# Last round of an MLP: a plain chunk ahead of the pair of a seven-product and a plain chunk, and final norm's row loaded in the last chunk

## The chip, the cores and the metric

The kernel runs on one core of one Trainium2 chip. The metric is the device time of one execution in microseconds; times of a kernel are given as the median of three runs. The engines are TensorE (PE, matrix products; PEld are its weight loads), VectorE (DVE), ScalarE (ACT), GpSimd (POOL) and SyncE (SP), whose queue issues the transfers from and to HBM.

## The reference, cut to what matters

One decoder layer on 256 tokens of 2048 features in float32: two groups of attention heads, an output projection, and then an MLP of four times the width, with norms and residual adds. The change lies in the MLP and in the last norm:

```python
h = rms_norm(x, norm2_g[l])
x = x + jnp.square(jax.nn.relu(h @ w_mlp_in[l])) @ w_mlp_out[l]
...
return rms_norm(x, final_norm_g)
```

## The kernel before

All products are made with operands that are split into a high and a low part (float32r): hi x hi, lo x hi and hi x lo, three matrix instructions for one product. A weight block is loaded from HBM by SP into a buffer raw (1 MB, 512 rows of 512 columns; four buffers), and split in two *steps* of 256 rows each: ACT writes the high part whi (L252), DVE subtracts and writes the low part wlo (L253). The tiles for these parts come from a ring of five (wsplit has four, late5 the fifth), so that a split of a step can begin when PE has done the step five before it.

The weights are cut into *chunks* of 512 output columns. The MLP has four rounds (r = 0 to 3). In each, four chunks "u" (up projection, features on the partitions, L414) make 2048 hidden features, and four chunks "d" (down projection, d(r,0) to d(r,3)) multiply them by 2048 rows of w_mlp_out and add to the residual xs. A d chunk of eight steps is done in one of two ways:

- *plain*: product(), L397 to L399, into two accumulators "acc", one per token tile (128 tokens). There are four acc banks, so a chunk works in two while the two before are drained. drain_d adds them to xs on DVE (L808).
- as a *seven-product* (seven_products(), L457): a Strassen-like form of the 2 x 2 block product with seven products in place of eight. It needs sums and differences of the weights (L207, L222, L223 on DVE) and of the hidden activations (mix_activations and split_mixed, L743 to L746 and mix_hi, mix_lo), and all four banks called sc and tr. drain_seven takes it to xs in four parts, on slots 1, 3, 5 and 7 behind its end (L784 to L792 and L777); its copies tile, its both, fhi and flo and the mix_hi and mix_lo tiles lie in a pool "late".

One seven-product chunk, d(r-1,0), is woven into the four u chunks of the next round, a quarter (a *unit* of four steps near, first, odd, even) to each. d(r,1) is woven with the plain d(r,2) in the same way, four units of six steps: this is the *pair*. d(r,3) is plain. In the last round d(3,0) is plain too, since no u chunks follow.

The order of the steps is written out in the list steps (L147 to L158). A *slot* is half a step, 128 rows of the weights; side work is hung on slots with at(slot, function). e is the slot of a chunk's last step. When a slot's products are issued, run_side issues its side work, so on each engine the drains stand in the queue between the splits of the steps ahead. How far ahead the splits go is set by free_tiles and, near the end, by upto (L946); load_more keeps up to four raw buffers in use.

The last chunk, d(3,3), is written by last_chunk (L846): first all of token tile 0, then tile 1 in two halves of 256 columns. The high and low parts of its first three steps go to the tiles aT_hi and aT_lo, which the u chunks have done with. For the final norm each piece of xs is squared and summed on ACT when its last add is done (square_and_gain, L802), and multiplied by the gain row gf on DVE (put_gain, L820). load_gf (L757) closes the pool "late", takes gf (8 KB on each partition, the same 2048 values on all) in its place, and loads it on SP's queue; so it has to wait until the last readers of that pool are done. finish computes the norm's factor for a token tile from the sums (POOL for the power, L833), scales the tile on DVE and ACT (L841, L843), and sends it out on SP (L844).

In the last round before the change the order is: four u chunks with d(2,0); the pair d(3,1) and d(3,2); plain d(3,0); plain d(3,3). The drains of the pair, load_gf and put_gain for columns 512 to 1535 are hung on slots of d(3,0).

Of the kernel before, what the change touches and what calls it, by code (L numbers as in the profile page):

```python
# [28 lines left out]
CW = 512  # L29
# [45 lines left out]
def kernel(  # L75
# [51 lines left out]
    ROUNDS = D_FF // D_MODEL  # L127
# [8 lines left out]
    steps = [(ci, s, "") for ci in range(mlp0) for s in range(chunks[ci][6] // 2)]  # L136
# [4 lines left out]
    def plain(ci):  # L141
        return [(ci, s, "") for s in range(KT // 2)]

    def mixed(ci, unit, behind):
        b, a, t13, t24 = ((ci, 2 * unit, sub) for sub in ("near", "first", "odd", "even"))
        return [b, a, t13, behind[0], t24] + behind[1:]

    for r in range(ROUNDS):
        for c in range(4):
            mine = plain(index["u", (r, c)])  # L150
            steps += mine[:4] + (mixed(index["d", (r - 1, 0)], c, mine[4:]) if r else mine[4:])
        late = [index["d", (r, c)] for c in range(4)]
        if r < ROUNDS - 1:
            steps += plain(late[3])
        for unit in range(4):
            steps += mixed(late[1], unit, plain(late[2])[2 * unit:2 * unit + 2])
        if r == ROUNDS - 1:
            steps += plain(late[0]) + plain(late[3])  # L158

    last_slot = {chunks[ci][:2]: 2 * i + 1 for i, (ci, _, _) in enumerate(steps)}  # L160
    units = list(dict.fromkeys((ci, s // 2) for ci, s, _ in steps))
# [311 lines left out]
    def at(i, f, *a):  # L473
        side.setdefault(i, []).append((f, a))
# [293 lines left out]
    def drain_seven(r, c, ci, part):  # L768
# [28 lines left out]
        if r == ROUNDS - 1 and part % 2:  # L797
            square_and_gain(part // 2, cs, c)

    def square_and_gain(t, cs, n):  # L800
        unused = two.tile([P, CW], F32, name="nat")
        nc.scalar.activation(unused[:, :cs.stop - cs.start], xs[:, t, cs], AF.Square, accum_out=ssq3[:, t, n:n + 1])  # L802
        if n not in (1, 2):
            put_gain(t, cs)

    def add_down(acc, t, cs, n):

        nc.vector.scalar_tensor_tensor(  # L808
            xs[:, t, cs], acc[:, :cs.stop - cs.start], rstd2sq[:, t:t + 1], xs[:, t, cs], op0=ALU.mult, op1=ALU.add
        )  # L810
        if n is not None:
            if cs.stop < D_MODEL:
                square_and_gain(t, cs, n)
            else:
                unused = two.tile([P, CW], F32, name="nat")
                unused, xc, total = unused[:, :cs.stop - cs.start], xs[:, t, cs], ssq3[:, t, n:n + 1]
                nc.vector.tensor_tensor_reduce(unused, xc, xc, 1.0, 0.0, ALU.mult, ALU.add, total)

    def put_gain(t, cs):
        nc.vector.tensor_tensor(xs[:, t, cs], xs[:, t, cs], late_tiles["gf"][:, cs], op=ALU.mult)  # L820
# [51 lines left out]
    for ci, (what, key, *_rest) in enumerate(chunks[:-1]):  # L872
        e = last_slot[what, key]
        if what == "v":
            at(e, drain_v, key, ci)
            if key == 0:
                at(e + 2, forget_gates)
                at(e + 6, gate_sums)
                at(e + 4, rel_row)
                at(e + 5, rel_back)  # L880
                at(e + 55, rel_turn)
        elif what in "qk":
            for half in range(2):
                late = half if what == "k" else (2 if key else 8) + 5 * half
                at(e + late, drain_qk, key, what, ci, half)
            if what == "k":
                kind = groups[key][4]
                for h in range(4):
                    n = e + 6 + 7 * (h // 2)
                    if kind == 0:  # L890
                        at(n - 3, decay_of, groups[key][3] * 4 + h)
                    at(n, scores, key, h)
                for h in range(4):
                    at(e + 20 + 7 * (h // 2), values, key, h)
                for h in range(4):
                    at(e + 13 + 7 * (h // 2), turn_probs, key, h)
                if key % 2:
                    at(e + 33, group_norm, kind)
        elif what == "o":
            at(e, drain_o, *key, ci)  # L900
            if key[0] == 1:
                for n in range(2):
                    at(e + 2, to_features, 4 * key[1] + 2 * n, 16)
                if key[1] == 3:
                    at(e + 4, second_norm)
        elif what == "u":
            at(e, drain_u, key[1], ci)
            at(e + 2, mix_activations, key[1])
            at(e + 4, split_mixed, key[1])
        elif ci in seven:  # L910
            for part in range(4):
                at(e + 1 + 2 * part, drain_seven, *key, ci, part)
            if key[0] == ROUNDS - 1:
                at(e + 7, load_gf)
                for c in (1, 2):
                    for t in range(TB):
                        at(e + 11 + 2 * c + t, put_gain, t, slice(c * CW, (c + 1) * CW))
        else:
            at(e, drain_d, *key, ci)

# [31 lines left out]
    for i in range(final):  # L952
        if i == mlp_start:
# [3 lines left out]
            late = late_forms.enter_context(tc.tile_pool(name="late", bufs=1))  # L957
# [58 lines left out]
```

## Time and profile before

| | us |
|---|---|
| median of three runs | 1099.67 |
| the three runs | 1099.06, 1099.67, 1099.78 |
| profiled execution, its own time | 1097.77 |
| its span, first to last instruction | 1096.0 |
| PE busy in the span | 1080.1 |
| DVE busy | 800.7 |
| ACT busy | 604.1 |
| last round: last u product (995.42) to last chunk (1064.47) | 69.05 |
| last chunk: token tile 0 | 10.88 |
| last chunk: tile 1, two halves | 5.75 and 5.96 |
| from the last product to the end of the span | 8.94 |

Rows of a timeline have the start and the length of an instruction in us, the engine, the line, the operation, the tile written and the tiles read, the sizes, and in square brackets how long the engine was idle before it and who ended that. Rows of who waited for whom have the sum, the number and the longest of the waits. A row of "windows" has a stretch, its length and the busy time and instruction count of each engine in it, then the TensorE clock granted (1.00 is full) and the share and rate of the DMA engines.

### The profile page before, as it was taken

What the parts mean: (1) busy time and instruction counts of PE and PEld (TensorE: products, weight loads), DVE (VectorE), ACT (ScalarE), POOL (GpSimd) and SP (SyncE); (2) the same over time, 40 slices, a digit from 0 to 9 for tenths busy, and PEclk for the clock granted to TensorE, in tenths of its full rate; (3) what the DMA queues carried; (4) which work ended last, traced back from release to release, by engine and by line L of the source; (5) the groups of instructions that cost most, each with busy time, mean ns of one, the idle gap of its engine ahead of it and who ended that gap; (6) DMA issues with size and microseconds to landing.
All of it is one profiled execution on the core that took longest, in us unless ns stands there. A gap on an engine that the chain in (4) does not pass through costs nothing.

```text
span 1096.0 us, 19064 instructions
## 1 busy us (share of the span) xinstructions
PE 1080.1 (99%) x7877; PEld 1014.8 (93%) x7877; DVE 800.7 (73%) x1076; ACT 604.1 (55%) x821; POOL 27.9 (3%) x42
## 2 busy tenths in 40 slices
PE   9999999999999999999999999999999999998996
PEld 7999899998988899998999998999998899998886
DVE  6666756667576666578777789787778887779774
ACT  6455545546455565655546665546666556666541
POOL 0010200000001000000000000000000000000000
PEclk9999999999999999999999999999999999999999
DMA  8665464655545567646766554675665666655642
GB/s 319 235 217 169 155 200 146 193 177 170 193 154 192 165 188 224 193 158 207 216 196 199 205 203 158 206 218 187 197 212 173 194 197 186 193 196 180 215 178 77
DMA packets 105395, 209.27 MB, mean 191 GB/s; under 512 B 3971, under 2 KB 5084, under 8 KB 105180
## 3 DMA queue, kind: packets, MB, share of 16 engines
q1 hardware_dynamic: 104412, 206.59, 57.7%
q8 instruction: 61, 1.00, 0.4%
q0 software_dynamic: 304, 1.06, 0.3%
q10 hardware_dynamic: 592, 0.40, 0.1%
q14 instruction: 26, 0.21, 0.1%
HBM read 205.93 MB, written 2.11 MB: 190 GB/s over the span
## 4 chain that ended last, share of the span: by engine, by line
PE 98%; ACT 0%; DVE 0%; DMA 0%; issue 0%; POOL 0%; ACTq 0%; DVEq 0%
PE acc L414 48%; PE acc L397 11%; PE acc L398 11%; PE acc L399 11%; PE sc L457 7%; PE tr L457 5%; PE tr L349 1%; PE sc L676 1%; PE sc L632 1%; PE tr L660 0%; DMA xs<-in_x_dram 0%; PE sc L628 0%; ACT whi L252 0%; PE sc L678 0%; PE sc L398 0%
## 5 line engine op out<-in xcount | busy, mean ns | idle before, releaser
L253 DVE TENSOR_TENSOR wlo<-raw,whi 128x1024 fp32r<-128x1024 f32 (+2 forms) x327 | 394.5, 1221 | 162.0 <-ACT whi L252 161.1
L252 ACT ACTIVATE whi<-raw 128x1024 fp32r<-128x1024 f32 (+2 forms) x328 | 339.2, 1050 | 228.3 <-PE acc L414 129.9
L414 PE MATMUL acc<-aT_hi,whi 128*128 128x256 f32 x1536 | 425.6, 277 | 0.0
L414 PE MATMUL acc<-aT_hi,wlo 128*128 128x256 f32 x1536 | 424.1, 276 | 0.0
L414 PE MATMUL acc<-aT_lo,whi 128*128 128x256 f32 x1536 | 423.9, 276 | 0.0
L414 PEld LDWEIGHTS acc<-aT_hi,whi 128*128 128x128 f32 x1536 | 288.1, 188 | 1.2 <-issue 0.9
L414 PEld LDWEIGHTS acc<-aT_lo,whi 128*128 128x128 f32 x1536 | 288.2, 188 | 0.3
L414 PEld LDWEIGHTS acc<-aT_hi,wlo 128*128 128x128 f32 x1536 | 288.1, 188 | 0.1
L397 PE MATMUL acc<-whi,big_hi 128*128 128x512 f32 (+1 forms) x414 | 160.2, 387 | 0.0
L398 PE MATMUL acc<-whi,big_lo 128*128 128x512 f32 (+1 forms) x414 | 159.9, 386 | 0.0
L399 PE MATMUL acc<-wlo,big_hi 128*128 128x512 f32 (+1 forms) x414 | 159.8, 386 | 0.0
L399 PEld LDWEIGHTS acc<-wlo,big_hi 128*128 128x128 f32 x414 | 78.1, 189 | 15.8
L398 PEld LDWEIGHTS acc<-whi,big_lo 128*128 128x128 f32 x414 | 78.1, 189 | 14.4
L397 PEld LDWEIGHTS acc<-whi,big_hi 128*128 128x128 f32 x414 | 78.1, 189 | 14.2
L218 ACT ACTIVATE whi<-both 128x1024 fp32r<-128x1024 f32 x56 | 59.7, 1066 | 49.0 <-DVE both L223 17.1
L219 DVE TENSOR_TENSOR wlo<-both,whi 128x1024 fp32r<-128x1024 f32 x56 | 68.3, 1220 | 4.7 <-ACT whi L218 3.8
L336 DVE TENSOR_TENSOR big_lo<-nat,big_hi 128x512 fp32r<-128x512 f32 x32 | 22.1, 692 | 42.3 <-ACT big_hi L335 42.3
L397 PE MATMUL acc<-whi,aT_hi 128*128 128x512 f32 (+1 forms) x144 | 51.7, 359 | 0.0
L398 PE MATMUL acc<-whi,aT_lo 128*128 128x512 f32 (+1 forms) x144 | 51.0, 354 | 0.0
L399 PE MATMUL acc<-wlo,aT_hi 128*128 128x512 f32 (+1 forms) x144 | 51.0, 354 | 0.0
L218 ACT ACTIVATE whi<-raw 128x1024 fp32r<-128x1024 f32 x28 | 29.6, 1056 | 11.6 <-PE sc L457 5.0
L335 ACT ACTIVATE mix_hi<-nat 128x512 fp32r<-128x512 f32 x32 | 18.5, 625 | 29.9 <-DVE nat L745 29.9
(212 smaller groups left out, 1359.5 us busy)
## 6 DMA issues: line engine op xcount, KB each, us to landing
raw<-in_w_mlp_in_dram SPq DMA_DIRECT2D x64, 1024.0 KB, 5.6
raw<-in_w_mlp_out_dram SPq DMA_DIRECT2D x64, 1024.0 KB, 5.1
raw<-in_w_in_dram SPq DMA_DIRECT2D x42, 1024.0 KB, 5.2
raw<-in_w_out_dram SPq DMA_DIRECT2D x16, 1024.0 KB, 5.1
raw<-in_w_in_dram SPq DMA_DIRECT2D x4, 1040.0 KB, 9.5
xs<-in_x_dram SPq DMA_DIRECT2D x3, 512.0 KB, 9.5
raw<-in_w_in_dram SPq DMA_DIRECT2D x2, 512.0 KB, 5.3
big_lo<-rel_d POOLq DMA_DIRECT2D x1, 1024.0 KB, 7.1
```

Source lines behind the costliest of these rows:

```text
L218: nc.scalar.activation(hi, src, AF.Copy)
L219: nc.vector.tensor_tensor(lo, src, hi.bitcast(F32), op=ALU.subtract)
L252: nc.scalar.activation(hi[:, :, c:c + step], t[:, :, c:c + step], AF.Copy)
L253: nc.vector.tensor_tensor(lo, t, hi.bitcast(F32), op=ALU.subtract)
L335: nc.scalar.activation(hi, src, AF.Copy)
L336: nc.vector.tensor_tensor(lo, src, hi.bitcast(F32), op=ALU.subtract)
L349: nc.tensor.transpose(p[:, j * SEQ + t * P:j * SEQ + (t + 1) * P], xs[:, t, c:c + P], ident)
L397: nc.tensor.matmul(acc, xh, hi[:, j, cols], start=go, stop=False, skip_group_check=True)
L398: nc.tensor.matmul(acc, xl, hi[:, j, cols], start=False, stop=False, skip_group_check=True)
L399: nc.tensor.matmul(acc, xh, lo[:, j, cols], start=False, stop=end, skip_group_check=True)
L414: nc.tensor.matmul(acc, w[:, j, b * P:(b + 1) * P], a[:, kt, :], start=kt == 0 and b % 2 == 0 and n == 0, stop=kt == kts - 1 and n == 2, s ...
L457: nc.tensor.matmul(acc, a[:, k, tokens], w[:, j, n * half:(n + 1) * half], start=fresh and x == 0, stop=s == KT // 2 - 2 and j == 1 and x ...
```

## The change

In the last round the plain chunk d(3,0) comes ahead of the pair, as d(r,3) does in the other rounds; the pair is followed by the last chunk at once. The pair's drains, which hang on slots behind its end, fall into the last chunk, and with them load_gf (slot e + 7, which is the fifth of the last chunk's sixteen slots for token tile 0). put_gain for columns 0 to 1535 of both token tiles, six calls, hangs on slots e + 13 to e + 18, the last six of those sixteen; d(3,0) is no longer multiplied by gf at its drain, since gf is not there yet. Nothing else is changed: the products, the transfers and their sizes are the same.

```diff
@@ the order of the steps
         late = [index["d", (r, c)] for c in range(4)]
-        if r < ROUNDS - 1:
-            steps += plain(late[3])
+        steps += plain(late[3 if r < ROUNDS - 1 else 0])
         for unit in range(4):
             steps += mixed(late[1], unit, plain(late[2])[2 * unit:2 * unit + 2])
         if r == ROUNDS - 1:
-            steps += plain(late[0]) + plain(late[3])
+            steps += plain(late[3])
@@ square_and_gain
-        if n not in (1, 2):
+        if n > 2:
             put_gain(t, cs)
@@ side work of a seven-product chunk
             if key[0] == ROUNDS - 1:
                 at(e + 7, load_gf)
-                for c in (1, 2):
+                for c in range(3):
                     for t in range(TB):
-                        at(e + 11 + 2 * c + t, put_gain, t, slice(c * CW, (c + 1) * CW))
+                        at(e + 13 + 2 * c + t if t == 0 or c < 2 else e + 18, put_gain, t, slice(c * CW, (c + 1) * CW))
```

The changed file is one line shorter, so its line numbers behind the list of steps are one lower than those of before.

On PE, where the last product of the last u chunk (L414; L413 after the change) is followed by the first d products of the last round. Before:

```order
L414 MATMUL acc<-aT_lo,whi 128x256
L414 MATMUL acc<-aT_hi,wlo 128x256
L457 MATMUL sc<-whi,big_hi 128x256
L457 MATMUL sc<-whi,big_lo 128x256
L457 MATMUL sc<-wlo,big_hi 128x256
```

After:

```order
L413 MATMUL acc<-aT_lo,whi 128x256
L413 MATMUL acc<-aT_hi,wlo 128x256
L396 MATMUL acc<-whi,big_hi 128x512
L397 MATMUL acc<-whi,big_lo 128x512
L398 MATMUL acc<-wlo,big_hi 128x512
```

The seven-product's first step, into an sc bank, stood there; now the plain chunk's first step, into acc banks.

On SP's queue, the end of the program (raw are weight blocks, gf is final norm's row, out the output). Before:

```order
L177 DMA raw_11181<-in_w_mlp_out_dram 128x4x512
L177 DMA raw_11232<-in_w_mlp_out_dram 128x4x512
L760 DMA gf_11265<-in_final_norm_g_dram 128x2048
L177 DMA raw_11277<-in_w_mlp_out_dram 128x4x512
L844 DMA out_0_dram<-xs_87 128x384
```

After:

```order
L176 DMA raw_11153<-in_w_mlp_out_dram 128x4x512
L176 DMA raw_11201<-in_w_mlp_out_dram 128x4x512
L176 DMA raw_11251<-in_w_mlp_out_dram 128x4x512
L759 DMA gf_11385<-in_final_norm_g_dram 128x2048
L843 DMA out_0_dram<-xs_87 128x384
```

The load of gf stood ahead of the last weight block; now it stands behind all of them, and only outputs follow.

On DVE, from the last drains of the pair to the add of the last chunk's token tile 0 (L808 with acc; L807 after). Before, where the rows begin in d(3,0):

```order
L792 TENSOR_TENSOR tr<-tr,copies 128x256
L777 SCALAR_TENSOR_TENSOR xs<-sc,rstd2sq,xs 128x512
L253 TENSOR_TENSOR wlo_11249<-raw,whi_11248 128x1024
L777 SCALAR_TENSOR_TENSOR xs<-tr,rstd2sq,xs 128x512
L253 TENSOR_TENSOR wlo<-raw,whi 128x1024
L253 TENSOR_TENSOR aT_lo<-raw,aT_hi 128x1024 x3
L253 TENSOR_TENSOR wlo<-raw,whi 128x1024
L820 TENSOR_TENSOR xs<-xs,gf 128x512 x4
L253 TENSOR_TENSOR wlo<-raw,whi 128x1024 x2
L808 SCALAR_TENSOR_TENSOR xs<-acc,rstd2sq,xs 128x512
```

After, where all of them but the splits of the first six steps (the first two rows) stand behind the pair's end:

```order
L252 TENSOR_TENSOR aT_lo<-raw,aT_hi 128x1024 x3
L252 TENSOR_TENSOR wlo<-raw,whi 128x1024 x3
L785 TENSOR_TENSOR tr<-tr,copies 128x256
L776 SCALAR_TENSOR_TENSOR xs<-sc,rstd2sq,xs 128x512
L807 SCALAR_TENSOR_TENSOR xs<-acc,rstd2sq,xs 128x512 x2
L252 TENSOR_TENSOR wlo_11350<-raw,whi_11349 128x1024
L776 SCALAR_TENSOR_TENSOR xs<-tr,rstd2sq,xs 128x512
L776 SCALAR_TENSOR_TENSOR xs<-sc,rstd2sq,xs 128x256
L252 TENSOR_TENSOR wlo<-raw,whi 128x1024
L791 TENSOR_TENSOR tr<-tr,copies 128x256
L776 SCALAR_TENSOR_TENSOR xs<-sc,rstd2sq,xs 128x512
L776 SCALAR_TENSOR_TENSOR xs<-tr,rstd2sq,xs 128x512
```

The next row there is put_gain, L819, six in a row, then the two sums and the add of tile 0. The first put_gain waits for gf; before, the four at that place came between splits, half a chunk behind the load.

## The prediction

> **What bounds the kernel now.** I read the page first: the span, the busy shares and the chain that ended last.
>
> ```profile
> span 1096.0 us, 19064 instructions
> PE 1080.1 (99%) x7877; PEld 1014.8 (93%) x7877; DVE 800.7 (73%) x1076; ACT 604.1 (55%) x821; POOL 27.9 (3%) x42
> PE 98%; ACT 0%; DVE 0%; DMA 0%; issue 0%; POOL 0%; ACTq 0%; DVEq 0%
> ```
>
> TensorE (PE) works nearly all the time and 98% of the last chain is PE. The change leaves the matrix products as they are, so it can only move two things: places where PE waits, and the stretch after the last product. The list of who waited for whom, for PE from 400 us to the end, has one row:
>
> ```profile
> PE tr L457 <- DVE xs L777: 3.3, 1, 3.3
> ```
>
> The timelines of PE and of DVE show where it is: in the last round, in the first unit of the pair.
>
> ```profile
> 998.04 0.28 PE L457 MATMUL sc<-wlo,mix_hi 128*128 128x256 f32 x1
> 1001.61 0.38 PE L457 MATMUL tr<-whi,mix_hi 128*128 128x256 f32 x1 [3.29 <-DVE xs L777]
> 1000.81 0.74 DVE L777 SCALAR_TENSOR_TENSOR xs<-tr,rstd2sq,xs 128x512 f32<-128x512 f32 x1
> ```
>
> The pair's seven-product takes over all four sc and tr banks from the seven-product that ran beside the last u chunks. Its last drain (L777) stands on DVE behind the drains and splits of that u chunk and ends at 1001.55; PE, wanting the last tr bank, sits for 3.29 us. Windows then price this and the end: stretch, length, PE busy (instructions), the same for PEld, DVE, ACT and POOL, the granted clock, DMA share, GB/s.
>
> ```profile
> 998.04:1001.61 3.57, 0.28 (x4) 0.08 (x2) 2.78 (x5) 2.52 (x3) 0.00 (x0) 1.00 0.00 0
> 1001.61:1005.48 3.87, 3.87 (x15) 3.43 (x15) 3.77 (x7) 2.64 (x4) 0.00 (x0) 0.56 0.78 269
> 824.55:888.28 63.73, 63.73 (x362) 55.94 (x361) 52.66 (x59) 36.25 (x43) 0.00 (x0) 1.00 0.61 197
> 995.42:1064.47 69.05, 65.75 (x362) 57.38 (x361) 56.73 (x66) 39.73 (x51) 0.00 (x0) 0.98 0.55 190
> 1064.47:1075.35 10.88, 10.88 (x49) 9.01 (x48) 7.70 (x11) 3.35 (x6) 0.00 (x0) 1.00 0.01 2
> 1075.35:1081.10 5.75, 5.75 (x49) 5.75 (x48) 4.10 (x10) 0.72 (x1) 1.34 (x2) 1.00 0.12 44
> 1081.10:1087.06 5.96, 5.92 (x50) 5.72 (x48) 1.13 (x4) 0.51 (x2) 0.00 (x0) 1.00 0.35 133
> 1087.06:1096.00 8.94, 0.00 (x0) 0.00 (x0) 3.29 (x10) 0.72 (x1) 1.08 (x2) 0.71 0.31 118
> ```
>
> **What the reorder removes.** The third and fourth rows are the same work, 362 PE instructions: a plain chunk and the pair. In round 2 (824.55 to 888.28) the plain chunk goes first, which is the order that the change gives to the last round; there PE is busy in all of the 63.73 us. In the last round the pair goes first and the stretch takes 69.05 us. The difference, 5.32 us, is the gain if the last round comes to run as round 2 does. It has two parts. The idle time is 1001.61 - 998.04 less a normal step of 0.12, 3.45 us. The rest, 1.87 us, is PE working at a granted clock of 0.56 in the 3.87 us behind the wait (and a hiccup before it). I take all of it: the drains that PE waited for get a whole plain chunk, which works in acc banks of its own, to finish in (two token tiles of 10.88 us, fifth row). As to what is late next: the plain chunk's banks and operands come as in round 2, where nothing waits.
>
> **What the reorder adds at the start of the pair.** The plain chunk's drain in the last round also squares its result on ACT, twice, and the pair's next ACT split is queued behind that. One such square and its read take 0.66 us (rows at 1044.05 and 1044.71 below), so 1.3 us, and the split also waits until the drain is through; it comes some 2 us later than in round 2. That split is for the last of the six steps of the pair's first unit. Two rows of the chain give the length of a unit, 10.49 us from first product to first product:
>
> ```profile
> 1011.41 1.42 PE sc L457 x12
> 1021.90 1.42 PE sc L457 x12
> ```
>
> The last step, 12 plain products, is a quarter of 10.88 us, 2.72; PE gets to it 7.8 us into the pair. So no cost; without that cover it would be those 2 us.
>
> **What it adds at the end.** Now the pair's drains, both its squares, the load of gf (final norm's row) and six put_gain stand inside the last chunk. I count from its first product, Tc (1064.47 in the trace of before). How the drains run behind a pair, before shows too: there another plain chunk follows, from 1042.71, with the same row of drains, squares and splits. The rows are from the timelines of PE, DVE, ACT and SP, with one on the weight loads' time to landing.
>
> ```profile
> 1042.71 0.39 PE L397 MATMUL acc<-whi,big_hi 128*128 128x512 f32 x1
> 1043.28 1.40 DVE L808 SCALAR_TENSOR_TENSOR xs<-acc,rstd2sq,xs 128x512 f32<-128x512 f32 x2
> 1044.05 0.63 ACT L802 ACTIVATE nat<-xs 128x512 f32<-128x512 f32 x1 [2.41 <-DVE xs L808]
> 1044.71 0.63 ACT L802 ACTIVATE nat<-xs 128x512 f32<-128x512 f32 x1
> 1046.42 1.23 DVE L253 TENSOR_TENSOR wlo<-raw,whi 128x1024 fp32r<-128x1024 f32 x1 [1.74 <-ACT whi L252]
> 1049.55 1.99 ACT L252 ACTIVATE whi<-raw 128x1024 fp32r<-128x1024 f32 x2
> 1050.63 1.22 DVE L253 TENSOR_TENSOR wlo<-raw,whi 128x1024 fp32r<-128x1024 f32 x1 [1.80 <-ACT whi L252]
> 1051.77 0.42 DVE L792 TENSOR_TENSOR tr<-tr,copies 128x256 f32<-128x256 f32 x1
> 1052.35 0.45 SPq L760 DMA_DIRECT2D gf<-in_final_norm_g_dram  x1
> DMA to landing us min/median/max: 5.0/5.0/5.0
> 1057.69 0.37 SPq L177 DMA_DIRECT2D raw<-in_w_mlp_out_dram  x1
> ```
>
> *The splits.* Two splits of the last chunk stand between the drains. The second is the tighter one: by these rows it ends at 1050.63 + 1.22 - 1042.71 = Tc + 9.1. Its step is the eighth; each step of the first token tile takes 10.88 / 8 = 1.36 us, so it begins at Tc + 9.5, and the low part is wanted two products later. PE does not wait. The margin is about 0.8 us, and being late costs what it is late by.
>
> *The load.* gf takes the place of the buffers that the seven-products used, the last reader of which is drain_seven's part 2 (L792). In before SP issues it at 1052.35, 9.64 us after the chunk began. In after, part 0 is done before the pair ends, so the first drains can start up to 0.95 us earlier (the second of the two at 1043.28 waited behind part 0, not for PE): issue between Tc + 8.7 and Tc + 9.6; I take 9.0. Nothing stands behind it on SP but the outputs, and no weight load: those come earlier. From issue to landing there is no row for gf alone. The nearest is the weight load of the same 1 MB that runs alone on the same queue (issued at 1057.69): 5.0 us. From above: beside another 1 MB the bytes of gf end by 1059.00, 6.65 us after issue.
>
> ```profile
> 1058.50:1059.00 0.50, 0.50 (x4) 0.42 (x3) 0.50 (x2) 0.50 (x1) 0.00 (x0) 1.00 0.89 135
> 1062.00:1062.50 0.50, 0.50 (x4) 0.42 (x3) 0.50 (x2) 0.10 (x1) 0.00 (x0) 1.00 0.21 74
> ```
>
> From below: the bytes of the load alone end in the second row, some 4.4 us after issue. So gf lands at Tc + 14.0 (13.1 to 16.3).
>
> *The queue behind it.* DVE is done with part 3 near Tc + 10.5 and meets the first put_gain, which waits for gf. Behind it in order are five more, then the whole finish of token tile 0, then the two adds of tile 1, the last of which opens the final chain.
>
> ```profile
> 1062.12 2.50 DVE L820 TENSOR_TENSOR xs<-xs,gf 128x512 f32<-128x512 f32 x4
> 1073.77 0.15 DVE L824 TENSOR_REDUCE ssq3s<-ssq 128x1 f32<-128x3 f32 x1
> 1073.95 0.15 DVE L825 TENSOR_SCALAR ssq3s<-ssq3s 128x1 f32<-128x1 f32 x1
> 1075.55 0.75 DVE L808 SCALAR_TENSOR_TENSOR xs<-acc,rstd2sq,xs 128x512 f32<-128x512 f32 x1 [1.45 <-PE acc L399]
> 1078.77 1.46 DVE L843 TENSOR_SCALAR xs<-xs,rstd,fi_u 128x384 f32<-128x384 f32 x3
> 1081.31 0.48 DVE L808 SCALAR_TENSOR_TENSOR xs<-acc,rstd2sq,xs 128x256 f32<-128x256 f32 x1 [1.07 <-PE acc L399]
> 1082.95 0.15 DVE L825 TENSOR_SCALAR ssq3s<-ssq3s 128x1 f32<-128x1 f32 x1
> 1087.06 0.48 DVE L808 SCALAR_TENSOR_TENSOR xs<-acc,rstd2sq,xs 128x256 f32<-128x256 f32 x1 [3.96 <-PE acc L399]
> ```
>
> Four put_gain in 2.50 us, one alone 0.69, make 0.60 each: six, 3.62. The two sums: 1073.77 to 1074.10, 0.33. Tile 0 from its add to its last scaling: 1075.55 to 1080.23, 4.68, less 0.06 of overlap, 4.62. Tile 1's first half with its gain and sums: 1081.31 to 1083.10, 1.79. Together 10.36 us. The last add may thus start at 14.0 + 10.36 = Tc + 24.36. In before it starts at 1087.06 - 1064.47 = Tc + 22.59, set by PE, with DVE idle for 3.96 us before it. It comes 1.77 us late (0.87 to 4.07 for the landings above), and the 8.94 us behind it stay.
>
> **The sum.** -5.32 + 1.77 = -3.55 us. The profiled execution took 1097.77 us, its span 1096.0 and 1.77 around it; it would become 1094.22. The median of the three runs is 1099.67, 1.90 above the profiled one; I take the difference over: 1096.1 us.
>
> **A rule to weigh.** The trace has 5.0 us for 1 MB from SP. The Trainium skill, "DMA: Bandwidth & Descriptors", section "Bandwidth" (its table "Measured"), gives 6.15 us of data movement for 1 MB issued from GpSimd. By that the load would land 1.15 us later and the sum be 1097.2, an estimate; no run shows that path, and the row decides here.
>
> **Rivals.**
>
> *The low clock is not always there* (0.12). The 1.87 us beside the idle time hang on the granted clock of 0.56 in one profiled execution, behind an idle stretch of only 3.29 us. If the timed runs do not have it, the gain is 3.45: 1099.67 - 3.45 + 1.77 = 1098.0. For it: the profiled run is no timed run. Against: the three times lie within 0.72 us, so they all have it or none has. The Trainium skill, "TensorE: Matmul & The Clock Gate", Part 1, has the gate look at a free-running window of some 3.4 us, one idle window bringing half clock; by that an idle time of this length need not trip it every time. The trace shows one case in which it did.
>
> *gf comes slowly* (0.13 for 1.5 to 4 us more; 0.04 beyond). Every us of its landing is a us of the end from 12.2 us on (22.59 - 10.36). At 6.65 us the forecast becomes 1097.8; at 8 us, 1099.1. All is given back when it takes 8.55 us, and from there it is slower: at 12 us, 1103.1. For it: the row is read 128 times over from the same 8 KB, and no row shows that alone. Against: beside another load its bytes were there in 6.65 us.
>
> *The end costs nothing* (0.06): gf is early enough or DVE packs closer. 1099.67 - 5.32 = 1094.4.
>
> *The stall only moves* (0.03): PE waits as long at another place, say for the plain chunk's last operands, and the end costs 1.77: 1101.4. Round 2 speaks against it.
>
> **Chances and range.** The forecast itself (1095 to 1097.4) has 0.62. A measurement of this kernel can tell about 0.2%, 2.2 us, from no change: faster means below 1097.5. To that count the forecast, the free end and a part of the late load and the low clock: 0.75. Slower, above 1101.9, are the slow load's far end and the moved stall with a slow load: 0.04. The rest, 0.21, is the same. The range from 1094.5 (no cost at the end) to 1098.3 (no low clock, or a load of some 7 us) leaves out about 0.2.
>
> **What would show it.** In the trace of after: no PE wait at L457 in the last round, no stretch of granted clock 0.56 there, and 63.7 us from the last u product to the last chunk's first. At the end: the gf issue 9 us into the last chunk, DVE idle for 3 to 4 us before the first put_gain with the DMA as releaser, and the last add 1 to 3 us after PE's last product instead of at once. Wrong would be: the last add still released by PE, a wait of PE in the last chunk, or put_gain later than Tc + 16.

## The result, and the profile after

| us | before | after |
|---|---|---|
| median of five runs each | 1099.06 (1097.94 to 1099.78) | 1094.43 (1093.18 to 1095.18) |
| ratio, 95% interval | | 0.9957 [0.9942, 0.9972] |
| profiled execution, its own time | 1097.77 | 1095.18 |
| its span | 1096.0 | 1093.4 |
| first d product of the last round | 995.42 | 997.18 |
| from there to the last chunk's first product (Tc) | 69.05 | 63.74 |
| last add, from Tc | 22.59 | 23.38 |
| from the last add to the end of the span | 8.94 | 9.10 |

The changed kernel is faster by 4.6 us, 0.43% (0.28 to 0.58%). The two profiled executions differ by only 2.6 us. They can't be subtracted as a whole: the program ahead of the last round, which the change leaves alone, took 1.76 us longer in the profiled run of after (997.18 against 995.42). Three experiments below (e5, e6 and e7) deal with that. From the first d product to the end it is 100.58 us before and 96.22 after, 4.36 less: -5.31 for the stretch, +0.79 for the late add, +0.16 behind it.

The page of after, with the span, the busy shares and the last chain:

```profile
span 1093.4 us, 19064 instructions
PE 1079.8 (99%) x7877; PEld 1014.8 (93%) x7877; DVE 800.3 (73%) x1076; ACT 604.2 (55%) x821; POOL 27.9 (3%) x42
PE 95%; DVE 2%; DMA 1%; ACT 1%; issue 1%; POOL 0%; ACTq 0%; DVEq 0%; SPq 0%
```

PE's busy time is nearly that of before since two changes nearly cancel: the stretch has 2.01 us less of it (65.75 before, 63.74 now), and the slower start adds 1.76. PE's share of the last chain went from 98% to 95%: DVE, ACT and a DMA now stand on it. In the list of who waited for whom no row of PE is left from 400 us on. The windows of after, the stretch and then the last chunk (columns as before: length, PE, PEld, DVE, ACT, POOL, granted clock, DMA share, GB/s):

```profile
997.18:1060.92 63.74, 63.74 (x363) 55.94 (x361) 55.45 (x62) 39.05 (x48) 0.00 (x0) 1.00 0.54 182
1060.92:1083.50 22.58, 22.55 (x145) 20.48 (x143) 14.64 (x28) 5.79 (x13) 1.34 (x2) 1.00 0.16 58
```

PE is busy in all of the 63.74 us at full granted clock; the stretch of 0.56 is gone. At the end of the program the chain of waits runs through the load, in two of its rows:

```profile
1069.51 4.61 DMA gf<-in_final_norm_g_dram
1074.14 3.70 DVE xs L819 x6
```

And the timelines of PE, SP and DVE show the last chunk from its first product to the last add:

```profile
1060.92 0.39 PE L396 MATMUL acc<-aT_hi,big_hi 128*128 128x512 f32 x1
1060.51 1.39 DVE L807 SCALAR_TENSOR_TENSOR xs<-acc,rstd2sq,xs 128x512 f32<-128x512 f32 x2
1068.99 0.42 DVE L791 TENSOR_TENSOR tr<-tr,copies 128x256 f32<-128x256 f32 x1
1069.51 0.34 SPq L759 DMA_DIRECT2D gf<-in_final_norm_g_dram  x1
1070.10 0.75 DVE L776 SCALAR_TENSOR_TENSOR xs<-tr,rstd2sq,xs 128x512 f32<-128x512 f32 x1
1074.14 3.70 DVE L819 TENSOR_TENSOR xs<-xs,gf 128x512 f32<-128x512 f32 x6 [3.29 <-DMA gf<-in_final_norm_g_dram]
1083.19 0.28 PE L398 MATMUL acc<-wlo,big_hi 128*128 128x256 f32 x1
1084.30 0.47 DVE L807 SCALAR_TENSOR_TENSOR xs<-acc,rstd2sq,xs 128x256 f32<-128x256 f32 x1
```

The read of copies (L791) ends the use of the pool "late", and SP issues gf 0.52 us after its start, Tc + 8.59. The bytes are there 4.61 us later, DVE has been idle for 3.29 us by then, and from the first put_gain to the last add it works off its queue in 10.16 us. The last add starts at Tc + 23.38. It has no releaser in brackets: PE's last product started at 1083.19 and was done by 1083.47; in before this add had waited 3.96 us for PE.

### The profile page after: what moved, and what is told of

Read it like the earlier page. It is cut to its first block, busy times and chain, and to the rows that moved or that the text cites. A ratio compares the mean times of both kernels' runs of the same rounds, so it can differ in the third digit from the quotient of the medians.

```text
span 1093.4 us, 19064 instructions
## 1 busy us (share of the span) xinstructions
PE 1079.8 (99%) x7877; PEld 1014.8 (93%) x7877; DVE 800.3 (73%) x1076; ACT 604.2 (55%) x821; POOL 27.9 (3%) x42
## 4 chain that ended last, share of the span: by engine, by line
PE 95%; DVE 2%; DMA 1%; ACT 1%; issue 1%; POOL 0%; ACTq 0%; DVEq 0%; SPq 0%
PE acc L413 48%; PE acc L396 10%; PE acc L397 10%; PE acc L398 10%; PE sc L456 7%; PE tr L456 5%; PE tr L348 1%; PE sc L675 1%; DVE wlo L252 1%; PE sc L631 1%; PE tr L659 0%; DMA xs<-in_x_dram 0%; DMA gf<-in_final_norm_g_dram 0%; DVE xs L819 0%; ACT whi L251 0%
## 5 line engine op out<-in xcount | busy, mean ns | idle before, releaser
L413 PE MATMUL acc<-aT_hi,whi 128*128 128x256 f32 x1536 | 426.5, 278 | 0.0
L413 PE MATMUL acc<-aT_lo,whi 128*128 128x256 f32 x1536 | 424.4, 277 | 0.0
L413 PE MATMUL acc<-aT_hi,wlo 128*128 128x256 f32 x1536 | 424.4, 277 | 0.0
L413 PEld LDWEIGHTS acc<-aT_hi,whi 128*128 128x128 f32 x1536 | 288.7, 188 | 1.3 <-issue 0.6
L413 PEld LDWEIGHTS acc<-aT_lo,whi 128*128 128x128 f32 x1536 | 288.6, 188 | 0.3
L413 PEld LDWEIGHTS acc<-aT_hi,wlo 128*128 128x128 f32 x1536 | 288.4, 188 | 0.0
```

Of the source, the lines that this page charges most:

```text
L413: nc.tensor.matmul(acc, w[:, j, b * P:(b + 1) * P], a[:, kt, :], start=kt == 0 and b % 2 == 0 and n == 0, stop=kt == kts - 1 and n == 2, s ...
```

## Experiments

The theory: the reorder removes the wait for the last tr bank and the low clock behind it, and what it gives back is the landing of gf alone, one for one. The rivals: the gain or the loss has another source (the low clock absent in timed runs; DVE's packing rather than the load). Times stand beside the median of before on the same chip in the same hours: 1099.36 (21 runs) for the first four, 1098.97 (15 runs) for the last three.

**e1_gain_early: the load no longer waits for the pool.** gf goes into one of the weight buffers raw, which come free earlier, and is loaded at the pair's end.

```diff
 def load_gf
-        late_forms.close()
-        gf = late_tiles["gf"] = ctx.enter_context(tc.tile_pool(name="gain", bufs=1)).tile([P, D_MODEL], F32, name="gf")
+        spare = wraw.tile([P, 4, CW + NH], F32, name="raw")
+        gf = late_tiles["gf"] = spare.rearrange("p k c -> p (k c)")[:, :D_MODEL]
 side work of a seven-product chunk
-                at(e + 7, load_gf)
+                at(e, load_gf)
+                at(e + 7, late_forms.close)
```

> The changed kernel with one thing altered: gf is loaded into the weight buffer whose block (the last chunk's first) has been split, so it waits for that split and no longer for the pair's drains. Theory (the reorder removes 5.3 us, and the wait for gf gives 0.8 us of it back): gf is issued some 6 us before the last chunk instead of 8.6 us into it, the first put_gain does not wait, the last add is released by PE again, 22.6 us after the last chunk's first product instead of 23.4; the kernel is 5.3 us faster than before, 0.8 us faster than the changed one. Rival (the end is late because DVE's queue is too long there, whoever brings gf): the last add stays at 23.4 us and the time at 4.6 us below before.

Measured: 1092.91 us (1092.56 to 1093.60, 5 runs), ratio to before 0.9945 [0.9933, 0.9958]. SP's and DVE's timelines (gf is called raw here; the first d product is at 995.53, Tc at 1059.27):

```profile
1053.43 0.34 SPq L759 DMA_DIRECT2D raw<-in_final_norm_g_dram  x1
1069.13 3.69 DVE L819 TENSOR_TENSOR xs<-xs,raw 128x512 f32<-128x512 f32 x6
1081.86 0.48 DVE L807 SCALAR_TENSOR_TENSOR xs<-acc,rstd2sq,xs 128x256 f32<-128x256 f32 x1 [2.48 <-PE acc L398]
```

The load is issued 5.84 us ahead of the last chunk, the six put_gain follow the drains without a wait, and the last add waits for PE again, at Tc + 22.59 as in before. The stretch stays 63.74. The time behind the last add is again 8.9 us. So all of the loss at the end was the load's.

**e2_drain_first: the old order, one drain moved.** In before, the last part of the drain of d(2,0) is hung one slot earlier; the rest is as it was.

```diff
-                at(e + 1 + 2 * part, drain_seven, *key, ci, part)
+                at(e + min(1 + 2 * part, 6 if key == (ROUNDS - 2, 0) else 7), drain_seven, *key, ci, part)
```

> The kernel before, with the order of the chunks as it was; only the last part of the drain of d(2,0) is hung one slot earlier, so that on DVE it stands ahead of the drain of the last u chunk and one split instead of behind them. Theory (PE's stall is one tr bank whose drain stands too far back in DVE's queue): the add ends near 998.2 in the old trace's time instead of 1001.55, PE waits 0.2 us or not at all instead of 3.3, the clock stays at 1.00, and the kernel is about 5 us faster than before, with nothing lost at the end. Rival (the pair is too dense for DVE and ACT right behind the u chunks, so that it needs a plain chunk ahead of it): PE waits elsewhere in the pair's first unit and less than 2 us are won.

Measured: 1093.29 us (1092.99 to 1094.33, 5 runs), ratio 0.9951 [0.9937, 0.9964]. In before these three splits stood ahead of the drain at 1000.81:

```profile
997.50 0.68 DVE L336 TENSOR_TENSOR big_lo<-nat,big_hi 128x512 fp32r<-128x512 f32 x1
998.72 0.69 DVE L336 TENSOR_TENSOR big_lo<-nat,big_hi 128x512 fp32r<-128x512 f32 x1 [0.53 <-ACT big_hi L335]
999.66 1.23 DVE L253 TENSOR_TENSOR wlo<-raw,whi 128x1024 fp32r<-128x1024 f32 x1 [0.26 <-ACT whi L252]
```

In e2 DVE's timeline, then PE's, reads:

```profile
997.79 0.75 DVE L777 SCALAR_TENSOR_TENSOR xs<-tr,rstd2sq,xs 128x512 f32<-128x512 f32 x1
998.46 1.28 DVE L336 TENSOR_TENSOR big_lo<-nat,big_hi 128x512 fp32r<-128x512 f32 x2
999.85 1.23 DVE L253 TENSOR_TENSOR wlo<-raw,whi 128x1024 fp32r<-128x1024 f32 x1
```

```profile
998.22 0.28 PE L457 MATMUL sc<-wlo,mix_hi 128*128 128x256 f32 x1
998.60 0.38 PE L457 MATMUL tr<-whi,mix_hi 128*128 128x256 f32 x1
```

The drain stands ahead of three splits instead of behind them, starts at 997.79 instead of 1000.81, and PE goes on at 998.60, a quarter of a microsecond late. No wait of PE is listed. The stretch is 64.33 us, 0.6 above that of round 2, and nothing is lost at the end (last add at Tc + 22.59). So the wait came from the place of one DVE instruction in its queue; but for the 0.6 us, whose source no run shows, the order of the chunks matters only through it.

**e3_gain_twice: the load takes twice as long.** In the changed kernel gf is loaded twice in a row into the same tile.

```diff
-        nc.sync.dma_start(
-            gf, bass.AP(tensor=final_norm_g.tensor, offset=final_norm_g.offset, ap=[[0, P], [1, D_MODEL]])
-        )
+        for _ in range(2):
+            nc.sync.dma_start(
+                gf, bass.AP(tensor=final_norm_g.tensor, offset=final_norm_g.offset, ap=[[0, P], [1, D_MODEL]])
+            )
```

> The changed kernel with gf loaded twice into the same tile, the second load behind the first, so that it lands about 4.6 to 5 us later. Theory (the wait for gf sets the end, one for one): the last add comes 4.6 to 5 us later, the kernel is 4.6 to 5 us slower than the changed one, about as long as before. Rival (DVE has slack behind the first put_gain): less than 3 us.

Measured: 1098.24 us (1097.10 to 1099.90, 11 runs), ratio 0.9992 [0.9983, 1.0001]. Two rows of DVE's timeline, Tc being 1059.02:

```profile
1076.53 3.70 DVE L820 TENSOR_TENSOR xs<-xs,gf 128x512 f32<-128x512 f32 x6 [7.57 <-DMA gf<-in_final_norm_g_dram]
1086.70 0.47 DVE L808 SCALAR_TENSOR_TENSOR xs<-acc,rstd2sq,xs 128x256 f32<-128x256 f32 x1
```

The first put_gain comes at Tc + 17.51 instead of 13.22, 4.29 later, and the last add at Tc + 27.68 instead of 23.38, 4.30 later. The time rose by 3.8 us. Both are below the 4.6 to 5 us that were expected: the second load took 4.28 us (issued at 1072.25) where the first alone takes 4.6, and the time behind the last add was 8.63 us instead of 9.10. The rival, less than 3 us, is out: in this trace the later landing came back whole at the end, and 4.3 us more take back nearly the whole gain of the reorder.

**e4_fill_stall: PE kept busy while it waits.** In before, 24 unused products (128x256, into a free acc bank) stand right ahead of the product that waits. Their results are read by nobody.

```diff
+        if key_of(ci) == (ROUNDS - 1, 1) and begin and sub == "odd":
+            accs[ci + 1] = [psum.tile([P, CW], F32, name="acc", bufs=4) for _ in range(TB)]
+            fill = (accs[ci + 1][0], mix_hi[:, k1, upper], hi[:, j, :half])
...
+            if n == 1 and sub == "odd" and begin and key_of(ci) == (ROUNDS - 1, 1):
+                for _ in range(24):
+                    nc.tensor.matmul(fill[0][:, :half], fill[1], fill[2], start=True, stop=True)
```

> The kernel before with 24 products more, whose result nobody reads, right ahead of the product that waits in the last round; they go to an acc bank that is free and take 24 x 0.118 = 2.8 us, less than the wait. Theory (the half clock behind the wait comes from PE's being idle for 3.3 us): the idle time shrinks to some 0.5 us, the granted clock stays at 1.00 behind it, and the kernel is 1.7 to 1.9 us faster than before although PE does more. Rival (the slow products come from what DVE and ACT do there, or the clock falls in the profiled run alone): no change within 0.5 us.

Measured: 1096.55 us (1095.91 to 1098.42, 11 runs), ratio 0.9982 [0.9973, 0.9991], 2.0 us faster than before by the ratio (1.0 to 3.0); the medians differ by 2.8. PE's timeline, and the window of 3.87 us behind the wait:

```profile
999.58 0.28 PE L466 MATMUL sc<-wlo,mix_hi 128*128 128x256 f32 x1
999.70 2.89 PE L464 MATMUL acc<-whi,mix_hi 128*128 128x256 f32 x24
1003.16 0.39 PE L466 MATMUL tr<-whi,mix_hi 128*128 128x256 f32 x1 [0.58 <-DVE xs L786]
```

```profile
1003.16:1007.03 3.87, 3.87 (x21) 3.40 (x22) 3.77 (x7) 2.64 (x4) 0.00 (x0) 1.00 0.74 271
```

The waiting product starts just as late, 1003.16 - 999.58 less 0.12 = 3.46 us. But the 3.87 us behind it now have 21 products at a granted clock of 1.00, where before had 15 at 0.56. The stretch takes 67.53 us, 1.52 less than in before. So PE's idleness itself brings the low clock. The timed runs have it too: each has its mean granted clock on record, 0.995 or 0.996 in all 21 runs of before and 0.998 in all 11 here. The 3.41 us at half clock in the trace of before make 0.0016 of that mean. It also holds the half clock behind the last product (5.2 us of the span in the trace of before, 4.0 here), so a single run settles little, but all of them together do.

**e5_warm_before, e6_warm_after and e7_warm_gain: where the 1.76 us ahead of the change come from.** PE's timeline at the program's start, first in before, then in after:

```profile
1.18 3.60 PE L316 MATMUL sc<-nat 128*128 128x512 bf16 x8 [1.18 <-DVE relx L293]
6.09 0.55 PE L349 MATMUL tr<-ident,xs 128*128 128x128 f32 x3 [1.11 <-DMA xs<-in_x_dram]
7.09 0.71 PE L414 MATMUL acc<-aT_hi,whi 128*128 128x256 f32 x4
7.64 0.63 PE L414 MATMUL acc<-aT_lo,whi 128*128 128x256 f32 x4
```

```profile
1.18 3.60 PE L315 MATMUL sc<-nat 128*128 128x512 bf16 x8 [1.18 <-DVE relx L292]
6.11 0.90 PE L348 MATMUL tr<-ident,xs 128*128 128x128 f32 x3 [1.12 <-DMA xs<-in_x_dram]
7.73 1.42 PE L413 MATMUL acc<-aT_hi,whi 128*128 128x256 f32 x4
8.94 1.05 PE L413 MATMUL acc<-aT_lo,whi 128*128 128x256 f32 x4
```

The same instructions behind the same idle time run at full pace in one and at about half pace in the other, until about 10.2 us. Eight unused products stand ahead of them in both (first row), to wake the engine. Three kernels have eleven: before, after, and e1.

```diff
-WARM, WARM2 = 8, 3
+WARM, WARM2 = 11, 3
```

> The kernel before with eleven unused products at the very start of PE instead of eight, so that the 1.11 us in which PE sits without work ahead of 6.09 us is filled. Theory: the six profiled runs so far begin in two ways. In four (before, and the first three experiments) the products behind that idle time go at full pace from about 6.1 us and the first d product of the last round comes at 995.3 to 995.6; in two (after, and the one with the wait filled) PE goes at half pace until about 9.5 us (the first three transposes take 0.90 us instead of 0.55, twelve u products 2.34 instead of 1.57) and everything behind is 1.7 us later. If the idle time lets PE fall back to half pace in most of the timed runs of before, that is the better part of the 1.6 to 1.9 us by which their median stands above the profiled run, and this kernel is 1 to 1.7 us faster than before (1097.6 to 1098.4) with a smaller scatter than the 2.9 us of before. Rival: the scatter comes from elsewhere, or a longer warm-up only delays the first transposes: no change, 1099.0 to 1099.8 beside 1099.4.

> The changed kernel with the same eleven products at the start. Its own profiled run had the slow start (first d product at 997.18) and took 1095.18, the median of five 1094.43. Theory of the two starts: every run of this kernel has the fast start, so 1093.2 to 1093.8. Rival (scatter from elsewhere): 1094.4. In the trace the stretch stays at 63.7 us and the last add at 23.4 us into the last chunk in either case, since nothing of the change is touched.

> The changed kernel with the early load of gf and the same eleven products at the start: the fastest version that the theories give. Its profiled run without them had the fast start already and took 1092.57, median 1092.91. Theory of the two starts: 1092.3 to 1092.8, all runs within 0.8 us. Rival (the longer warm-up delays the first transposes): 1093 or above.

| | median, us | runs | ratio to before | profiled, own time | first d product | last add, from Tc |
|---|---|---|---|---|---|---|
| e5_warm_before | 1097.94 (1096.22 to 1098.73) | 11 | 0.9989 [0.9981, 0.9998] | 1097.51 | 995.42 | 22.59 |
| e6_warm_after | 1093.26 (1093.11 to 1093.61) | 5 | 0.9950 [0.9936, 0.9964] | 1093.61 | 995.45 | 23.56 |
| e7_warm_gain | 1092.38 (1092.29 to 1092.88) | 5 | 0.9943 [0.9930, 0.9955] | 1092.29 | 995.50 | 22.59 |

In all three profiled runs PE is at full pace by 5.8 us. All three medians lie below those of the kernels with eight products, but clear of noise this is for e5 alone (its interval ends below 1); the intervals of e6 and after, and of e7 and e1, overlap. For e6 and e7 the expected times and scatter came true (0.50 and 0.59 us). For e5 they did in part: 1.03 us faster by the medians, the small end of what was expected, and its scatter of 2.5 us is no smaller than the 2.4 of the 15 runs of before beside it. The expectation's mechanism is not what the traces show: PE does not fall back to half pace in the idle time, it has not yet come up in the slow starts (last section). What else moves the runs of e5 and before stays open. All 15 runs of before have a mean granted clock of 0.995 or 0.996, so there a missing low clock is hardly it. In e5 seven runs have 0.995 or 0.996 and four 0.997, among them the two fastest (1096.22 and 1096.38); those two may have been without the low clock, which is not shown. With eleven products in both, the change is worth 1097.94 - 1093.26 = 4.68 us and the late load 1093.26 - 1092.38 = 0.88, where the traces have 23.56 - 22.59 = 0.97. e7 is the fastest version of all.

## Why the prediction was right in its mechanism and wrong in its number

The result lies below the low end of the range, by 0.07 us, and 1.67 below the forecast. Step by step:

*The gain of the reorder* (-5.32, from round 2): right. The last round took 63.74 us, a gain of 5.31, and no new wait took the place of the old one. That the start of the pair costs nothing was right with it. Its two parts were sized nearly as they are. The 3.45 of idleness is 3.46 in e4. Of the other 1.87, the low clock is 1.71, half of the 3.41 us that this window of before has at half clock (columns as in the prediction):

```profile
1002.00:1005.41 3.41, 3.41 (x13) 3.02 (x13) 3.34 (x5) 2.57 (x4) 0.00 (x0) 0.50 0.85 298
```

e4, without the low clock, won 1.52 of the 1.87. What the rest is, between 0.16 and 0.35 us, no run shows; e2, without the wait and without the low clock, is still 0.6 slower than round 2.

*The low clock is not always there*: the rival fell for before. Filling the idle time would not have made timed runs 2.0 us faster if they had no low clock, and no run of before has a mean clock above 0.996. The Trainium skill, "TensorE: Matmul & The Clock Gate", Part 1, would let an idle time of 3.3 us bring half clock in some runs and not in others; the profiled run with its 0.56 and the gain of e4 show that it mostly does here, and the open scatter of e5 leaves room for some without it.

*No cost in PE's last chunk*: right. PE's last product starts 22.27 us after Tc in before, in after and in all the first four experiments. The other rivals fell too: gf did not come slowly, the end was not free, and no wait of PE came up elsewhere.

*The cost at the end* (+1.77): this is the first step that failed, not in its mechanism but in each of its three sizes, all to the same side. "I take 9.0" for the issue was 8.59, just outside the stated 8.7 to 9.6: the two adds at L807 began 0.41 us ahead of Tc, where those of before began 0.57 us behind it, so the drains came 0.98 us earlier instead of at most 0.95. "gf lands at Tc + 14.0" rested on 5.0 us, a weight load's time, and gf alone took 4.61, so the first put_gain came at 13.22. The queue behind it, 10.36 as the sum of single rows, took 10.16. Together 0.98 us: Tc + 23.38 instead of 24.36, a cost of 0.79. The landing was inside its bounds (13.1 to 16.3), near the lower one; the cost was not, its stated low end being 0.87, since the queue was shorter too. The Trainium skill's 6.15 us of data movement for 1 MB ("DMA: Bandwidth & Descriptors", section "Bandwidth") lies further off; it is for the path from GpSimd. The prediction says that no run shows that path, but each trace has one load of 1 MB issued from GpSimd (big_lo from rel_d, beside weight loads), which took 7.1 us from issue to landing in before and 8.1 in after. That the load's time decides from there on was right: e3 added 4.29 to the landing and 4.30 to the end.

*"I take the difference over"* (+1.90 from the profiled time to the median): this is the second step that failed, and it weighs as much. The profiled run of before had the fast start, and its median stood 1.90 above it, in five runs 1.29. After's profiled run has 1.76 more at the start; with before's start it would be 1093.42, and its median stands 1.01 above that. So 0.89 of the 1.67 came from the offset and 0.80 from the end (0.98 less the 0.16 that the tail grew; rounding is the rest). Of the 0.89, 0.61 is only the median of before itself, 1099.67 in three runs and 1099.06 in five: from the latter the same sum gives 1095.5. The offset is no constant of the kernel: with eleven products at the start it was 0.43 in e5, -0.35 in e6 and 0.09 in e7.

*The range.* Its low end was the case of no cost at the end, 1094.4, which stood on the same 1099.67. It held the unknown landing, but nothing for the offset.

## What to carry to other kernels

A wait of TensorE for a bank can come from the place of one drain in VectorE's queue: before an order of chunks is turned round, try to move that drain (e2 won 0.49% by moving it one slot, the reorder 0.43%, and the intervals overlap). An idle time of PE can cost more than its length, because of the clock behind it: here 3.45 us of idleness brought 1.71 us more. A load that takes the place of a pool waits for that pool's last reader; look for a buffer that comes free earlier, and when a profiled time is carried over to a median, first compare the parts that the change does not touch.

## What the runs showed of the hardware that was not expected

In every trace PE starts at half pace: the first unused products (128x512) stand 0.43 us apart from start to start, where the last ones in e6 and e7 stand 0.22 apart. What differs is when full pace comes. The clock record that each trace holds begins with the change to full: at 5.31 us in before, 4.17, 4.51 and 4.31 in e1, e2 and e3, but at 10.22 in after and 9.69 in e4; with eleven products at 5.80, 4.02 and 3.93 in e5, e6 and e7. So the slow start is a late warm-up and no fall back in the idle time. Before, e1, e2 and e3 reached the last round at 995.3 to 995.6 us, after and e4 at 997.0 to 997.2. Two rows of the chain, the first twelve u products of before and of after, have it:

```profile
7.29 1.57 PE acc L414 x12
```

```profile
8.29 2.34 PE acc L413 x12
```

The granted clock in the windows reads 1.00 in both: for 8 to 10 us PE issues 16 products in before and 10 in after.

```profile
8.00:10.00 2.00, 2.00 (x16) 1.65 (x15) 1.30 (x5) 0.69 (x3) 0.00 (x0) 1.00 1.05 398
```

```profile
8.00:10.00 2.00, 2.00 (x10) 1.92 (x9) 1.21 (x3) 0.13 (x1) 0.00 (x0) 1.00 1.06 386
```

The column reads 1.00 also where a trace holds no clock record yet, so it does not show a slow start; the lengths of equal instructions do. The Trainium skill, "TensorE: Matmul & The Clock Gate", Part 1, says that the gate's window runs free of the kernel's start, so that the same kernel warms up sooner or later; the two starts of the same code agree with that, and with three more products at the start full pace came by 5.8 us in all three traces. In the last round the half clock of before lasted 3.41 us (1002.00 to 1005.41), and that of e5, behind the same wait, 3.41 us as well (1002.49 to 1005.90).

The load of gf, 1 MB that reads the same 8 KB for every partition, was as quick as a load of 1 MB of weights: 4.61 us alone in after and 4.78 in e6 beside 5.0.
